# Weaving two self attentions with dense products in a written TensorE order

## The chip, the cores and the metric

The kernel runs on one core of a Trainium2 chip. The metric is the time of one execution on the device in microseconds (us). PE is TensorE (matrix products and transposes), DVE is VectorE, ACT is ScalarE, POOL is GpSimd, SP is the engine whose queue issues most of the DMAs. PSUM is the memory into which PE writes; it has eight banks of 128 x 512 float32 elements.

## The reference

Two transformer layers run one after the other on 512 tokens of width 1024. The first has a feed-forward part, a mixer with three branches, and another feed-forward part; the second layer (a recurrent mixer and a feed-forward part) is not touched. The change lies in the first mixer:

```
(fq, fk, fv, ff, dq, dk, dv, iq, ik, iw, mq, g) = split(rmsnorm(h) @ w_in)
# branch 0, "fox": 8 heads of 64, causal, with forget gates
s = fq . fk / 8 + c_query - c_key,  c = cumsum(log_sigmoid(ff + b_forget))
o_a = softmax(causal(s)) @ fv                    # fq, fk are normalized by head
# branch 1, "dsa": 8 heads of 64, one key and value for all heads
score = sum over 8 heads of iw * relu(iq . ik)   # the indexer
o_b = softmax(dq . dk / 8 over the 128 best keys of each query) @ dv
# branch 2, memory: 4 heads of 128 over 256 memory rows
o_c = softmax(mq . km / sqrt(128)) @ vm
gates = sigmoid(g)                               # 3 x 1024
h = h + (sum over n of gates[n] * (o[n] @ w_branch[n])) @ w_out
```

All inputs and outputs are float32.

## The kernel before, in words

Activations lie feature-major: a tile is 128 features by 512 tokens, and the model's 1024 features are eight such tiles. Every dense product is made of three PE products, because float32 is split into a high and a low part that PE takes in its rounded form fp32r: high x high, high x low, low x high (`mm3`, L163, L168, L169). Weights come by DMA as a `raw` block of 512 KB; ACT rounds it to `whi` (L157), DVE subtracts to get `wlo` (L158), and PE uses such a block in 24 products of 128 x 512. `gemm_fm` runs such products over blocks of 256 output features; its results go into two PSUM banks in turn (tag `g`).

The mixer (`Mix1.run`) goes through these stages: a small product for keys and scalars; the indexer's queries `iq`; the indexer (`pix` products, whose sums DVE gathers); the memory attention; the products for `fv`, `fq`, `fk`; the fox attention; the search for the 128 best keys (`selected`, 48 pairs of MAX8 and MATCH_REPLACE8 on DVE); the memory branch (gates, then the projection, `branch(2)`); the product for `dq` with its norm and rotation (`rope`); the dsa attention; the other two branches; the output product.

An attention is cut into 16 units: four chunks of two heads, times four blocks of 128 queries (`qb`). A unit with `w` = 128 (qb + 1) keys does, for each of its two heads: scores (L584 and L585); a DVE instruction that adds the mask and takes the row maximum (L986 or L1008); the exponential with its row sum on ACT (L689); a reciprocal on DVE (L690); the multiplication by it on POOL (L691); one to four transposes on PE (L679) into the PSUM tile `pt`; a copy on ACT (L681). Then PE multiplies by the values (L697), one product of 64 output rows for each head and block, into the PSUM tile `po`.

A score is two products. The query tile `st` holds a head's high part in the head's own 64 partitions and its low part in the other 64 (`stacked`). The key tile `kh` holds the high part twice. So the first product uses all 128 rows of PE's array. The second multiplies the high part of the query by the low part of the key `kl` and uses 64 rows:

```python
own, w = slice(p * 64, p * 64 + 64), max(w, 256)
self.nc.tensor.matmul(ps[:, :w], q, keys[0][:, :w], start=True, stop=False)
self.nc.tensor.matmul(ps[:, :w], q[own], keys[1][own, :w], start=False, stop=True)
```

The order of the instructions on every engine is made by a list scheduler from the order of the program's text, priorities, its own estimates of durations and the free buffers: it may put PE products of a later stage between those of an attention. Each engine then runs its list in order and waits on semaphores. PSUM banks of the mixer: two for dense products (`g`), one general (`a`), three for scores (`s`), one for `pt` (`p`), one for `po` (`o`).

Of the kernel before, what the change touches and what calls it, by code (L numbers as in the profile page):

```python
# [19 lines left out]
D = 1024  # L20
# [7 lines left out]
class K:  # L28
# [142 lines left out]
    def gemm_fm(self, w, c0, ncols, x, evac, kmax=4, after=None, then=iter(())):  # L171

        nk = len(x)
        for g in range(0, ncols, 256):
# [3 lines left out]
            for k0 in range(0, nk, kmax):  # L180
                kk = min(kmax, nk - k0)
                hi, lo = self.wload([(w[k0 * 128:(k0 + kk) * 128, c0 + g:c0 + g + gc], gc)], kk, gc)
                for (m, mc), ps in zip(ms, pss):
                    for k in range(kk):
                        xh, xl = x[k0 + k]
                        self.mm3(ps[:mc], hi[:, k, m:m + mc], lo[:, k, m:m + mc], xh, xl,
                                 k0 + k == 0, k0 + k == nk - 1, after if k0 + k == 0 else None)
                    if k0 + kk == nk:
                        evac((g + m) // 128, ps[:mc])
                next(then, None)  # L190
# [320 lines left out]
class Mix1:  # L511
# [54 lines left out]
    def doubled(self, x, new, lo):  # L566
# [3 lines left out]
        his = []  # L570
# [9 lines left out]
    def score(self, ps, q, p, keys, w):  # L580
# [25 lines left out]
    def head_stats_turned(self, chunks, heads, width, s):  # L606


        nc, k = self.nc, self.k
        per = 128 // width  # L610
# [3 lines left out]
        for i, c in enumerate(chunks):  # L614
            ps, sq = k.ps("tq", "s"), k.tmp("hq")
            for b in range(NB):
# [3 lines left out]
                                    mybir.AxisListType.X, ALU.add)  # L620
        yv, rt = y.rearrange("p (b h) -> p b h", b=NB), self.rt.unsqueeze(2).to_broadcast([128, NB, heads])
# [5 lines left out]
        return yv  # L627
# [22 lines left out]
    def head_norm_rows(self, chunks, y, gcol):  # L650

# [13 lines left out]
        nc.vector.tensor_sub(z[32:32 + n], ps[:n], z[:n].bitcast(F32))  # L665
        for i, x in enumerate(chunks):
# [4 lines left out]
            else:  # L671
                nc.vector.scalar_tensor_tensor(x, x, gcol, pb, op0=ALU.mult, op1=ALU.mult)

    def transposed(self, p, nb, s):

        nc, k = self.nc, self.k
        pt = k.ps("pt", "p")
# [29 lines left out]
    def run(self):  # L707
# [67 lines left out]
        scores, mq = [], []  # L775
        steps = self.indexer(iq, ik, scores, 4)
        k.gemm_fm(win, 2768, 512, y, raw_evac(mq), then=steps)
        for _ in steps:
            pass
        om = self.mem_attention(mq, self.head_stats_turned(mq, 4, 128, "hm"))  # L780

        fvt = k.sp.tile([128, NB, 512], F32, name="fv")
        k.gemm_fm(win, 1024, 512, y, self.turned_evac(fvt, R))
        fv = [fvt[:, b] for b in range(NB)]
        fq, fk = [], []
        k.gemm_fm(win, 0, 512, y, raw_evac(fq))
        st = self.head_stats_turned(fq, 8, 64, "hs")

        def norm():
            for _ in range(3):  # L790
                yield
            self.head_norm_rows(fq, st, k.c("fqg"))
            yield

        k.gemm_fm(win, 512, 512, y, raw_evac(fk), then=norm())
        self.head_norm_rows(fk, self.head_stats_turned(fk, 8, 64, "hs"), None)
        self.forget()
        of = self.fox(fq, fk, fv)
        bias = self.selected(scores)

        merged = [None] * DC
        self.branch(2, om, merged)

        dq = []
        k.gemm_fm(win, 1544, 512, y, raw_evac(dq, k.tmp))

        rq = self.head_stats_turned(dq, 8, 64, "hm")
        nc.vector.tensor_scalar(k.c("rot"), k.c("rot"), k.c("dqg"), None, op0=ALU.mult)
        nc.vector.tensor_scalar(self.cos, self.cos, k.c("dqg"), None, op0=ALU.mult)
        dq = [self.stacked(t, lambda s: k.slot(s, F32R)) for t in map(self.rope, dq)]  # L810
        od = self.dsa(dq, dk, bias, rq)

        self.branch(0, of, merged)
        self.branch(1, od, merged)
# [83 lines left out]
    def indexer(self, iq, ik, scores, n):  # L898
# [10 lines left out]
        for qb in range(1, NB):  # L909
            w = (qb + 1) * 128  # L910
            acc = k.slot("ix")[:, :w]
            for hh in range(8):
                c, p = hh // 2, hh % 2
                ps = k.ps("pix", "s")[:, :w]
                self.score(ps, iq[c][p][:, qb * 128:(qb + 1) * 128], p, ik, w)
# [11 lines left out]
    def selected(self, scores):  # L927

        k, nc = self.k, self.nc
        bias = [k.c("cmask")]  # L930
        for acc in scores:
            for _ in range(TOPK // 8):
                m8 = k.small("m8", [128, 8], bufs=6)
                nc.vector.max(m8, acc)
                nc.vector.match_replace(acc, m8, acc, TAKEN)
            nc.vector.tensor_scalar(acc, acc, 0.5 * TAKEN, MASK, op0=ALU.is_gt, op1=ALU.mult)
            bias.append(acc)
        return bias
# [18 lines left out]
    def fox(self, fq, fk, fv):  # L957
        k, nc = self.k, self.nc
        out = []

        def made(c):
            return (self.stacked(fq[c], lambda s: k.tmp(s, F32R)),
                    self.doubled(fk[c], lambda s: k.slot(s, F32R), k.tmp("kl", F32R)))

        ahead = made(0)
        for c in range(4):
            po = k.ps("po", "o")
            (q2, (k2, kl)), ahead = ahead, made(c + 1) if c < 3 else None
            nc2 = []
            for p in range(2):  # L970
                nct = k.tmp("nct", tag="nct")
                nc.sync.dma_start(nct, self.nc_rows[2 * c + p:2 * c + p + 1, :].to_broadcast([128, T]))
                nc2.append(nct)

            for qb in reversed(range(NB)):
                w = (qb + 1) * 128
                d = slice(w - 128, w)
                pts = []
                for p in range(2):
                    nct = nc2[p]  # L980
# [828 lines left out]
```

## Time and profile before

| | |
|---|---|
| median of 3 runs | 2288.93 us (2285.36 to 2290.96) |
| the profiled execution | 2286.21 us, its span 2284.5 us |
| busy share of the span | PE 97%, DVE 57%, ACT 38%, POOL 15% |
| mean granted PE clock | 0.990 of full speed |
| chain of work that ended last | PE 87%, DVE 5%, POOL 4% |
| DMA | 202.39 MB, mean 89 GB/s |

The span is from the first to the last instruction; the execution's own time is 1.7 us more. A matrix product's row in the trace lasts longer than the distance to the next product's start, since products are pipelined, so PE shows as busy while products follow each other at any distance below their length. What a product costs is read from start to start. In the stretch from 449.7 us (the first rotation of the mixer) to 939.5 us (where the output product begins) lie all the stages named above from the indexer on.

### The profile page before, as it was taken

Reading aid. Unit: us, or ns where it says so; the run is one execution under the profiler, and the core shown is the slowest. Engines: PE = TensorE matmul, PEld = TensorE weight load, DVE = VectorE, ACT = ScalarE, POOL = GpSimd, SP = SyncE. Lnnn points to the kernel's source line nnn. Section 1 sums busy time; section 2 is a strip of 40 time slices with the busy share of each in tenths; the row PEclk is TensorE's granted clock in tenths of the full one; section 3 lists DMA queues with packets and bytes.
Section 4 is the critical chain, followed back from the end, with each engine's and each line's share of the span. In section 5 each row is a group of like instructions: output and inputs, shape, how many; then the busy total and the mean of one; then the engine's idle time right before and its main releaser. Section 6 shows DMA issues by size and latency. Waiting matters only on the chain.

```text
span 2284.5 us, 27935 instructions
## 1 busy us (share of the span) xinstructions
PE 2224.8 (97%) x10700; PEld 1772.9 (78%) x10700; DVE 1305.4 (57%) x2210; ACT 877.1 (38%) x1485; POOL 346.6 (15%) x349
## 2 busy tenths in 40 slices
PE   8999999999999999999999998999999998999998
PEld 7788888768767578888888877778777787888887
DVE  4544433589763644544443348985888725877623
ACT  4432222345373542332322235543433534444321
POOL 0110100111040421101111012370222200000000
PEclk9999999999999999999999999999999999999999
DMA  4333333312312113333332332331121223333232
GB/s 150 93 111 102 98 100 117 105 44 58 93 56 74 37 47 111 114 90 96 100 94 95 116 108 66 93 109 30 56 73 48 74 93 120 93 95 99 94 99 94
DMA packets 198509, 202.39 MB, mean 89 GB/s; under 512 B 19556, under 2 KB 184063, under 8 KB 198375
## 3 DMA queue, kind: packets, MB, share of 16 engines
q1 hardware_dynamic: 197607, 198.12, 28.9%
q0 software_dynamic: 768, 2.49, 0.4%
q8 instruction: 84, 1.38, 0.3%
q14 instruction: 50, 0.41, 0.1%
HBM read 192.70 MB, written 7.88 MB: 88 GB/s over the span
## 4 chain that ended last, share of the span: by engine, by line
PE 87%; DVE 5%; POOL 4%; issue 1%; ACT 1%; DMA 1%; SPq 0%; POOLq 0%; DVEq 0%; ACTq 0%
PE pg L169 23%; PE pg L163 23%; PE pg L168 23%; PE pd L1739 2%; PE pd L1738 2%; PE pd L1737 2%; PE po L697 1%; POOL blocks L1349 1%; PE pt L679 1%; POOL xt L1348 1%; PE pss L585 1%; DVE wlo L158 1%; PE pyd L1536 1%; PE pss L584 1%; PE tr L1126 1%
## 5 line engine op out<-in xcount | busy, mean ns | idle before, releaser
L163 PE MATMUL pg<-yh,whi 128*128 128x512 f32 x1856 | 737.1, 398 | 4.0 <-ACT yh L219 2.3
L169 PE MATMUL pg<-yh,wlo 128*128 128x512 f32 x1856 | 736.2, 397 | 1.3 <-DVE wlo L158 1.1
L168 PE MATMUL pg<-yl,whi 128*128 128x512 f32 x1856 | 734.8, 396 | 0.0
L158 DVE TENSOR_TENSOR wlo<-raw,whi 128x1024 fp32r<-128x1024 f32 x341 | 422.7, 1240 | 529.2 <-ACT whi L157 518.6
L157 ACT CAST whi<-raw 128x1024 fp32r<-128x1024 f32 x349 | 362.0, 1038 | 701.4 <-PE pg L168 511.6
L169 PEld LDWEIGHTS pg<-yh,wlo 128*128 128x128 f32 x1856 | 351.2, 189 | 78.7 <-issue 5.0
L163 PEld LDWEIGHTS pg<-yh,whi 128*128 128x128 f32 x1856 | 351.4, 189 | 78.0 <-issue 6.0
L168 PEld LDWEIGHTS pg<-yl,whi 128*128 128x128 f32 x1856 | 351.2, 189 | 72.6 <-issue 3.1
L163 PE MATMUL pg<-hidh,whi 128*128 128x512 f32 x352 | 138.9, 394 | 0.0
L169 PE MATMUL pg<-hidh,wlo 128*128 128x512 f32 x352 | 138.1, 392 | 0.0
L355 POOL TENSOR_TENSOR hp<-ut,sg 128x512 f32<-128x512 f32 x44 | 73.3, 1666 | 422.7 <-DVE ut L353 398.0
L168 PE MATMUL pg<-hidl,whi 128*128 128x512 f32 x352 | 136.8, 389 | 0.0
L211 ACT CAST hidh<-hp 128x512 fp32r<-128x512 f32 x44 | 27.3, 620 | 142.4 <-POOL hp L355 142.3
L169 PEld LDWEIGHTS pg<-hidh,wlo 128*128 128x128 f32 x352 | 66.1, 188 | 15.4
L1696 DVE SCALAR_TENSOR_TENSOR fo<-ft,fcw,fo 128x511 f32<-128x511 f32 x88 | 65.8, 749 | 21.2 <-ACT fo L1693 20.0
L168 PEld LDWEIGHTS pg<-hidl,whi 128*128 128x128 f32 x352 | 66.1, 188 | 14.6
L163 PEld LDWEIGHTS pg<-hidh,whi 128*128 128x128 f32 x352 | 66.3, 188 | 13.1
L212 DVE TENSOR_TENSOR hidl<-hp,hidh 128x512 fp32r<-128x512 f32 x44 | 30.4, 691 | 79.5 <-ACT hidh L211 79.5
L1737 PE MATMUL pd<-whi,hidh 128*128 128x512 f32 x176 | 69.5, 395 | 0.0
L1738 PE MATMUL pd<-whi,hidl 128*128 128x512 f32 x176 | 69.5, 395 | 0.0
L1739 PE MATMUL pd<-wlo,hidh 128*128 128x512 f32 x176 | 69.3, 397 | 0.0
L346 DVE TENSOR_TENSOR gt<-pg,R 128x512 f32<-128x512 f32 x44 | 30.3, 692 | 55.2 <-PE pg L169 55.2
(501 smaller groups left out, 3067.7 us busy)
## 6 DMA issues: line engine op xcount, KB each, us to landing
raw<-in_w_in SPq DMA_DIRECT2D x100, 512.0 KB
raw<-in_ffn_w_gate SPq DMA_DIRECT2D x40, 512.0 KB
raw<-in_ffn_w_up SPq DMA_DIRECT2D x40, 512.0 KB
raw<-in_ffn_w_down SPq DMA_DIRECT2D x40, 512.0 KB
raw<-in_w_up SPq DMA_DIRECT2D x40, 512.0 KB
raw<-in_w_out SPq DMA_DIRECT2D x24, 512.0 KB
raw<-in_w_down SPq DMA_DIRECT2D x22, 512.0 KB
raw<-in_w_branch SPq DMA_DIRECT2D x12, 512.0 KB
```

The costliest lines, as they stand in the source:

```text
L157: nc.scalar.copy(hi, raw)
L158: (self.lo or nc.vector).tensor_sub(lo, raw, hi.bitcast(F32))
L163: first = mm(out, whi, xhi, start=start, stop=False)
L168: mm(out, whi, xlo, start=False, stop=False)
L169: mm(out, wlo, xhi, start=False, stop=stop)
L212: nc.vector.tensor_sub(lo, x, hi.bitcast(F32))
L346: nc.vector.tensor_mul(gt, ps, R)
L355: nc.gpsimd.tensor_mul(p, ut, sg[m])
L1696: nc.vector.scalar_tensor_tensor(o[:, s:], t[:, :T - s], k.fcw[:, j:j + 1], o[:, s:], op0=ALU.mult, op1=ALU.add)
L1737: nc.tensor.matmul(pss[b], xh[:, s], hi[:, i], start=st, stop=False)
L1738: nc.tensor.matmul(pss[b], xl[:, s], hi[:, i], start=False, stop=False)
L1739: nc.tensor.matmul(pss[b], xh[:, s], lo[:, i], start=False, stop=sp)
```

## The change

- `score` uses all 128 rows in its second product too. For this `doubled` makes two tiles `kl` for a chunk of keys, one for each head, and copies the low part into the other 64 partitions (on ACT). The indexer's and dsa's keys had both halves filled already.
- `gemm_steps` yields after every three products (one `mm3`), so that dense products can be handed out in small steps.
- The stages before the fox attention come in another order: `mq`, then `fk`, `fq`, `fv`, with the memory attention handed out in steps among them; `forget` moves ahead of `fk`.
- The units of fox and dsa form one list of 32. Inside a block marked `manual_schedule` the PE keeps the order of the text: for each unit the first head's transposes, one step (three products), the second head's transposes, the scores of the next unit, two steps, the unit's values, three steps, and two (fox) or three (dsa) steps more. The other engines are still ordered by the list scheduler. The steps are taken from the memory branch, `dq`, branch 0 and the gates of branch 1.
- The norm, rotation and splitting of `dq` are handed out between units 12 and 16. The two heads' `pt` tiles go to the banks `p` and `a`. Score tiles `s` get four buffers in place of three.

```diff
+    def gemm_steps(self, w, c0, ncols, x, evac, kmax=4, after=None):
...
+                        if k0 + kk == nk and k == kk - 1:
+                            evac((g + m) // 128, ps[:mc])
+                        yield m == ms[-1][0] and k == kk - 1
...
+    def doubled(self, x, new, newlo):
...
         for p in range(2):
-            t = new("kh")
+            t, lo = new("kh"), newlo("kl")
             own, other = (slice(o, o + 64) for o in (p * 64, 64 - p * 64))
             nc.scalar.copy(t[own], x[own])
+            nc.vector.tensor_sub(lo[own], x[own], t[own].bitcast(F32))
             nc.scalar.copy(t[other], t[own].bitcast(F32))
-            nc.vector.tensor_sub(lo[own], x[own], t[own].bitcast(F32))
-            his.append(t)
-        return his, lo
+            nc.scalar.copy(lo[other], lo[own].bitcast(F32))
+            out.append((t, lo))
+        return out
...
-        own, w = slice(p * 64, p * 64 + 64), max(w, 256)
...
+    def score(self, ps, q, keys, w):
...
+        w = max(w, 256)
         self.nc.tensor.matmul(ps[:, :w], q, keys[0][:, :w], start=True, stop=False)
-        self.nc.tensor.matmul(ps[:, :w], q[own], keys[1][own, :w], start=False, stop=True)
+        self.nc.tensor.matmul(ps[:, :w], q, keys[1][:, :w], start=False, stop=True)
...
+        def products():
+            yield from self.branch(2, om, merged)
+            yield from k.gemm_steps(win, 1544, 512, y, raw_evac(dq, k.tmp))
+            yield from self.branch(0, of, merged)
+            for g in range(0, D, 256):
+                yield from self.gates(1, g, "c", gates)
...
+            def between(i):
+                if i == 12:
...
+                    for _ in range(2):
+                        next(stats)
+                if i == 14:
+                    next(stats)
+                    rq.append(next(stats))
+                for c in {14: (0,), 15: (1,), 16: (2, 3)}.get(i, ()):
+                    dq2.append(self.stacked(dq[c], lambda s: k.slot(s, F32R)))
+                for c in {13: (0,), 14: (1,), 15: (2, 3)}.get(i, ()):
+                    self.rope(dq[c])
+            fill(4)
+            units[0].scores()
+            fill(6)
+            for i, u in enumerate(units):
+                u.turn(0)
+                fill(1)
+                u.turn(1)
+                if i + 1 < len(units):
+                    units[i + 1].scores()
+                for _ in range(4):
+                    next(top, None)
+                fill(2)
+                u.values()
+                fill(3)
+                between(i)
+                fill(2 if i < 16 else 3)
+            fill(1000)
+        for g in range(0, D, 256):
+            for _ in self.project(1, g, gates[g // 128:g // 128 + 2], od, merged):
+                pass
```

PE, inside the fox attention, before. `pss` are scores, `pt` transposes, `po` values, `pg` dense products (here of the memory branch):

```order
2659 L697 MATMUL po_4672<-pt_4730,fv 64x128
2660 L679 MATMUL pt_4753<-ct_base,s_4744 128x128 x3
2661 L584 MATMUL pss_4842<-kh_4668,st_4660 128x256
2662 L585 MATMUL pss_4842<-kl_4663,st_4660 128x256
2663 L168 MATMUL pg_5749<-oml_3830,whi_5752 128x512
2664 L169 MATMUL pg_5749<-omh_3829,wlo_5753 128x512
2665 L584 MATMUL pss_4885<-kh_4680,st_4673 128x512
2666 L679 MATMUL pt_4772<-ct_base,s_4763 128x128 x3
2667 L697 MATMUL po_4672<-pt_4757,fv 64x128
2668 L585 MATMUL pss_4885<-kl_4679,st_4673 128x512
2669 L163 MATMUL pg_5749<-omh_3902,whi_5752 128x512
2670 L584 MATMUL pss_4905<-kh_4684,st_4676 128x512
```

The same place in the changed kernel, from the second head's transposes of one unit to the first values:

```order
2685 L703 MATMUL pt_5168<-ct_base,s_5094 128x128 x4
2686 L591 MATMUL pss_5176<-kh_4703,st_4697 128x384
2687 L592 MATMUL pss_5176<-kl_4704,st_4697 128x384
2688 L591 MATMUL pss_5189<-kh_4709,st_4700 128x384
2689 L592 MATMUL pss_5189<-kl_4710,st_4700 128x384
2690 L163 MATMUL pg_5144<-omh_4653,whi_5148 128x512
2691 L168 MATMUL pg_5144<-oml_4654,whi_5148 128x512
2692 L169 MATMUL pg_5144<-omh_4653,wlo_5149 128x512
2693 L163 MATMUL pg_5145<-omh_4000,whi_5148 128x512
2694 L168 MATMUL pg_5145<-oml_4001,whi_5148 128x512
2695 L169 MATMUL pg_5145<-omh_4000,wlo_5149 128x512
2696 L721 MATMUL po_5222<-pt_5163,fv 64x128
```

Scores, transposes and values came singly, with one to four dense products between them, and a unit's values mostly in two parts (one product, then the rest); now both heads' scores stand together, six dense products follow, and a unit's values stand in one group.

ACT where the fox attention starts, before. `st` are split queries, `kh` keys, `s` exponentials, `pt` copies of transposes:

```order
325 L574 CAST kh_4668<-qk_4441 64x512
326 L575 CAST kh_4668<-kh_4668 64x512
327 L1051 ACTIVATE gate_5730<-gt_5728 128x512
328 L574 CAST kh_4680<-qk_4455 64x512
329 L689 ACTIVATE s_4696,den_4701<-s_4696,ng_4698 128x512
330 L157 CAST whi_5788<-raw_5786 128x1024
```

The same place in the changed kernel; `pt_4632` and `pt_4649` belong to the last unit of the memory attention, and `kl` to the first fox unit:

```order
317 L705 COPY pt_4632<-pt_4629 128x256
318 L582 CAST kh_4685<-kh_4685 64x512
319 L580 CAST kh_4691<-qk_3774 64x512
320 L705 COPY pt_4649<-pt_4646 128x256
321 L583 CAST kl_4686<-kl_4686 64x512
322 L582 CAST kh_4691<-kh_4691 64x512
323 L727 CAST omh_4653<-po_4483 128x512
324 L583 CAST kl_4692<-kl_4692 64x512
325 L580 CAST kh_4703<-qk_3788 64x512
```

The copies for the first fox scores stand behind the copies of the memory attention's last unit, and the first exponential (`s_4723`) stands another seven instructions further down, at number 332.

POOL where dsa starts, before. `qk` is a chunk of `dq` in its rotation, `s` the multiplication by the reciprocal:

```order
134 L550 TENSOR_TENSOR qk_6112<-qk_6112,ry_6206 128x512
135 L549 TENSOR_TENSOR qk_6126<-qk_6126,cos_3028 128x512
136 L550 TENSOR_TENSOR qk_6126<-qk_6126,ry_6218 128x512
137 L691 TENSOR_SCALAR s_6232<-s_6232,den_6237 128x128
138 L691 TENSOR_SCALAR s_6248<-s_6248,den_6253 128x128
```

And in the changed kernel, where `s_6226` and `s_6238` are the two heads of dsa's first unit:

```order
133 L715 TENSOR_SCALAR s_6226<-s_6226,den_6231 128x128
134 L555 TENSOR_TENSOR qk_6135<-qk_6135,cos_3028 128x512
135 L556 TENSOR_TENSOR qk_6135<-qk_6135,ry_6276 128x512
136 L555 TENSOR_TENSOR qk_6153<-qk_6153,cos_3028 128x512
137 L715 TENSOR_SCALAR s_6238<-s_6238,den_6243 128x128
138 L556 TENSOR_TENSOR qk_6153<-qk_6153,ry_6282 128x512
```

The last two rotations now stand between the two heads of dsa's first unit.

## Rows read from the trace of the kernel before

**Rows 1.** The page: busy us (share) x instructions; chain that ended last by engine.
```profile
PE 2224.8 (97%) x10700; PEld 1772.9 (78%) x10700; DVE 1305.4 (57%) x2210; ACT 877.1 (38%) x1485; POOL 346.6 (15%) x349
...
PE 87%; DVE 5%; POOL 4%; issue 1%; ACT 1%; DMA 1%; SPq 0%; POOLq 0%; DVEq 0%; ACTq 0%
```

**Rows 2.** Busy time by stage: from:to, length, engines' busy us, granted clock, DMA.
```profile
472.70:583.00 110.30, 110.13 (x521) 83.71 (x520) 102.97 (x279) 54.52 (x110) 10.23 (x19) 1.00 0.20 58
...
741.70:762.20 20.50, 16.95 (x58) 10.41 (x56) 17.90 (x35) 8.20 (x13) 8.62 (x7) 0.83 0.09 27
```

**Rows 3.** PE in order of time, indexer: start us, length us, instruction.
```profile
497.61 0.40 PE L584 MATMUL pix<-kh,st 128*128 128x512 f32 x1
497.94 0.49 PE L585 MATMUL pix<-kl,st 64*128 64x512 f32 x1
498.36 0.50 PE L168 MATMUL pg<-yl,whi 128*128 128x512 f32 x1
498.70 0.40 PE L169 MATMUL pg<-yh,wlo 128*128 128x512 f32 x1
498.93 0.40 PE L584 MATMUL pix<-kh,st 128*128 128x512 f32 x1
```

**Rows 4.** Groups of 64-row score products from 449 to 940 us.
```profile
L585 PE MATMUL pss<-kl,st 64*128 64x256 f32 (+2 forms) x64 | 27.2, 431 | 0.0
...
L585 PE MATMUL pix<-kl,st 64*128 64x256 f32 (+2 forms) x24 | 10.7, 445 | 0.0
```

**Rows 5.** PE in order of time, dense products 256 wide; and all LDWEIGHTS of L163.
```profile
111.12 0.28 PE L163 MATMUL pg<-my,whi 128*128 128x256 f32 x1
111.24 0.28 PE L168 MATMUL pg<-my,whi 128*128 128x256 f32 x1
...
L163 PEld LDWEIGHTS pg<-yh,whi 128*128 128x128 f32 x1856 | 351.4, 189 | 78.0 <-issue 6.0
```

**Rows 6.** PE in order of time, values of dsa (two records each).
```profile
779.88 0.43 PE L697 MATMUL po<-pt,tm 128*64 128x128 f32 x2
780.24 0.50 PE L169 MATMUL pg<-ofh,wlo 128*128 128x512 f32 x1
780.58 0.39 PE L163 MATMUL pg<-ofh,whi 128*128 128x512 f32 x1
...
785.49 1.09 PE L697 MATMUL po<-pt,tm 128*64 128x128 f32 x14
```

**Rows 7.** Waits of PE from 449 to 940 us: total, times, longest.
```profile
PE pss L584 <- DVE st L562: 1.8, 1, 1.8
PE rot L546 <- DVE ry L548: 1.7, 1, 1.7
...
PE pt L679 <- POOL s L691: 0.5, 1, 0.5
```

**Rows 8.** DVE and PE in order of time, first head of fox.
```profile
627.66 0.68 DVE L986 CUSTOM_DVE_ANT_0 s<-pss,nct 128x512 f32<-128x512 f32 x1
...
632.67 0.60 PE L679 MATMUL pt<-ct_base,s 128*128 128x128 f32 x4
```

**Rows 9.** Groups by shape from 449 to 940 us: busy us, mean ns, idle before.
```profile
L157 ACT CAST whi<-raw 128x1024 fp32r<-128x1024 f32 x57 | 59.8, 1050 | 120.0 <-PE pg L168 112.0 <-issue 8.0
...
L690 DVE RECIPROCAL den<-den 128x1 f32<-128x1 f32 x80 | 12.7, 159 | 12.2 <-ACT s L689 11.5
L550 POOL TENSOR_TENSOR qk<-qk,ry 128x512 f32<-128x512 f32 x8 | 12.6, 1579 | 12.3 <-DVE ry L548 3.4 <-DVE hst L230 3.4 <-DVE ng L1010 2.1
...
L691 POOL TENSOR_SCALAR s<-s,den 128x512 f32<-128x512 f32 x16 | 11.1, 692 | 13.1 <-DVE den L690 4.4 <-DVE ng L1010 3.0 <-DVE ng L987 1.5
...
L549 POOL TENSOR_TENSOR qk<-qk,cos 128x512 f32<-128x512 f32 x8 | 10.7, 1335 | 49.7 <-ACT hq L618 45.1 <-ACT st L561 2.9 <-PE rot L546 1.6
...
L689 ACT ACTIVATE s<-s,ng 128x512 f32<-128x512 f32 x8 | 5.8, 723 | 1.9 <-DVE ng L987 1.1 <-DVE den L690 0.8
...
L575 ACT CAST kh<-kh 64x512 fp32r<-64x512 f32 x8 | 4.9, 617 | 0.2
```

**Rows 10.** PE's granted clock in one stretch: length, PE busy, clock.
```profile
755.30:762.10 6.80, 6.80 (x14) 0.50 0.00 0
```

More of the change, by code (lines that the diff above doesn't have):

```diff
@@ L171, in gemm_fm @@
     def gemm_fm(self, w, c0, ncols, x, evac, kmax=4, after=None, then=iter(())):
+        for end in self.gemm_steps(w, c0, ncols, x, evac, kmax, after):
+            if end:
+                next(then, None)
+    def gemm_steps(self, w, c0, ncols, x, evac, kmax=4, after=None):
         nk = len(x)
@@ L613, in head_stats_turned @@
         xv = x.rearrange("p (b h) -> p b h", b=NB)
-        for i, c in enumerate(chunks):
+        for i in range(n_chunks):
+            c = chunks[i]
             ps, sq = k.ps("tq", "s"), k.tmp("hq")
@@ L774, in run, with first @@
             iq[i] = self.stacked(self.rope(iq[i]), new)
-        scores, mq = [], []
-        steps = self.indexer(iq, ik, scores, 4)
-        k.gemm_fm(win, 2768, 512, y, raw_evac(mq), then=steps)
+        scores, mq, om, fq, fk = [], [], [], [], []
+        fvt = k.sp.tile([128, NB, 512], F32, name="fv")
+        fv = [fvt[:, b] for b in range(NB)]
+        def first():
+            yield from self.indexer(iq, ik, scores, 4)
+            yield from self.mem_attention(mq, self.head_stats_turned(mq, 4, 128, "hm"), om)
@@ new lines, in after @@
+        def after(n, stats, chunks, gcol):
+            for _ in range(n):
+                next(steps, None)
+                yield
+            self.head_norm_rows(chunks, stats, gcol)
+            yield
+            while True:
+                next(steps, None)
+                yield
+        steps = first()
+        k.gemm_fm(win, 2768, 512, y, raw_evac(mq, lambda s: k.slot(s, tag="o")), then=steps)
+        self.forget()
+        k.gemm_fm(win, 512, 512, y, raw_evac(fk), then=steps)
+        st = self.head_stats_turned(fk, 8, 64, "hs")
@@ L778, in run @@
+        k.gemm_fm(win, 0, 512, y, raw_evac(fq), then=after(2, st, fk, None))
+        st = self.head_stats_turned(fq, 8, 64, "hs")
+        k.gemm_fm(win, 1024, 512, y, self.turned_evac(fvt, R), then=after(2, st, fq, k.c("fqg")))
         for _ in steps:
             pass
[L780 to L799, printed above, removed]
@@ L814, in run, with fill @@
-        self.branch(1, od, merged)
+        of, od, dq, gates, merged = [], [], [], [], [None] * DC
+        def products():
[4 more added lines that the diff above has]
+                yield from self.gates(1, g, "c", gates)
+        work = products()
+        def fill(n):
+            for _ in range(n):
+                next(work, None)
@@ new lines, in run @@
+        bias = [k.c("cmask")]
+        top = self.selected(scores, bias)
+        with self.tc.manual_schedule(engines={mybir.EngineType.PE}):
+            units = self.fox(fq, fk, fv, of)
+            dq2, rq = [], []
+            units += self.dsa(dq2, dk, bias, rq, od)
+            stats = self.stats_steps(dq, 8, 64, "hm", 4)
+            def between(i):
+                if i == 12:
+                    nc.vector.tensor_scalar(k.c("rot"), k.c("rot"), k.c("dqg"), None, op0=ALU.mult)
+                    nc.vector.tensor_scalar(self.cos, self.cos, k.c("dqg"), None, op0=ALU.mult)
+                    for _ in range(2):
[24 more added lines that the diff above has]
+            fill(1000)
@@ L955, in forget, with fox, at @@
         nc.sync.dma_start(self.nc_rows, c[:8])
-    def fox(self, fq, fk, fv):
+    def fox(self, fq, fk, fv, out):
         k, nc = self.k, self.nc
-        out = []
+        class Chunk:
+            pass
         def made(c):
[L962 to L969, printed above, removed]
+            x = Chunk()
+            x.q = self.stacked(fq[c], lambda s: k.tmp(s, F32R))
+            x.k = self.doubled(fk[c], lambda s: k.slot(s, F32R),
+                               (lambda s: k.hslot(s, F32R)) if c < 2 else (lambda s: k.slot(s, F32R)))
+            return x
+        ahead = {}
+        def at(c):
+            for i in (c, c + 1):
+                if i < 4 and i not in ahead:
+                    ahead[i] = made(i)
+            x = ahead[c]
+            x.nct, x.po = [], None
             for p in range(2):
@@ L972, in fox, with unit, scores @@
                 nc.sync.dma_start(nct, self.nc_rows[2 * c + p:2 * c + p + 1, :].to_broadcast([128, T]))
[L973 to L978, printed above, removed]
+                x.nct.append(nct)
+            return x
+        def unit(c, qb):
+            w = (qb + 1) * 128
+            d = slice(w - 128, w)
+            u = Chunk()
+            def scores():
+                x = u.x = at(c) if qb == NB - 1 else ahead[c]
+                u.s, u.pt = [], []
                 for p in range(2):
-                    nct = nc2[p]
+                    nct = x.nct[p]
                     nc.gpsimd.tensor_add(nct[:, d], nct[:, d], k.c("cmask"))
                     ps = k.ps("pss", "s")
-                    self.score(ps, q2[p][:, d], p, (k2[p], kl), w)
+                    self.score(ps, x.q[p][:, d], x.k[p], w)
                     s = k.tmp("s", tag="s")
```

152 lines of the change are left out of this document (88 added, 64 removed).

## The prediction, as it was made

> **What bounds the kernel now.** I read the page first. PE is busy in 2224.8 of 2284.5 us [rows 1], and the chain of work that ended last lies on it for 87% [rows 1]. So a gain has to come out of PE's own time, or out of the few places where PE waits. The next view is busy time by stage over the part that the change touches, 449.7 to 939.5 us. From 472.7 to 583.0 PE is busy for 110.13 of 110.30 us, and DVE for 102.97, because the search for the best keys runs there beside the indexer and the memory attention [rows 2]. The list of waits shows that PE hardly waits in this part: the longest waits from the fox attention on are 1.8 and 1.7 us, both just ahead of dsa [rows 7]. After them the granted clock is 0.50 for 6.8 us [rows 10], the lower level of 1.2 GHz.
>
> If PE neither waits nor is short of work, the question is what its busy time is made of. That takes the timeline, from start to start. Dense products of 512 columns follow each other at 0.23 us (the last two starts of [rows 3]). A score pair in the same stretch goes: 64-row product 0.33 us after the 128-row one, next product 0.42 us later, the one after it another 0.34 us later [rows 3]. Where 0.68 us would do for three products, these take 1.09. Each passage between products on 128 and on 64 rows thus costs about 0.2 us, half before and half behind it, and a pair in dense work has two. The trace counts the pair as busy all the while, so the page's 97% hides it.
>
> **The change part by part.**
>
> *Second score product on all rows.* Two passages a pair, 1.09 - 0.68 = 0.41 us; I take 0.39, a little under. There are 64 pairs in the two attentions and 24 in the indexer [rows 4]: 88 x 0.39 = 34 us. Some pairs share a passage with a neighbour that also changes the array's shape, so this is near the upper end; the lower is 25 us. That a full 128-row product of 256 columns can follow another with different weights at 0.12 us is shown by the memory product, although its weight load lasts 189 ns [rows 5]: loads are hidden.
>
> *Values in one group.* A lone value product (two records) holds PE for 0.36 us, and the second dense product behind it comes after 0.34 in place of 0.23 [rows 6]; seven last 1.09 against 0.43 for one, so a product itself is worth 0.11. The fixed part of a group is thus 0.36 - 0.11 + 0.11 = 0.36 us, and some 0.1 ahead of it. In the written orders values form 61 groups before and 32 after. 29 x 0.46 = 13 us is the upper end; about half of the old groups touch transposes or 64-row products, with which they share the passage, so I take 8, and 5 as the lower end.
>
> *Transposes.* Their number stays; more of the groups now stand between dense products. +1.5 us, from 0 to 3.
>
> *The passage to dsa.* Before, the chain norm, rotation, splitting of `dq` ran just ahead of the first dsa scores. It cost the waits of 1.8 and 1.7 us, one of 0.5 for POOL [rows 7], and the slow stretch: 6.8 us at half clock [rows 10] do the work of 3.4. The change spreads that chain over units 12 to 16. Removed: 1.8 + 1.7 + 0.5 + 3.4 = 7.4 us.
>
> Removed in all: 34 + 8 - 1.5 + 7.4 = 48 us. Now what is added.
>
> *DVE ahead of fox.* The search for keys still stands ahead of the first fox scores in DVE's list; handing it out four pairs a unit did not move it. In 472.7 to 583.0 PE's work shrinks by some 20 pairs x 0.39 = 8 us, to 102 us, while DVE keeps its 103 [rows 2]. DVE then has no slack and what is late is the norm of `fq`, so I add 3 us (0 to 8).
>
> *The start of fox.* PE's order is fixed there: last transposes and values of the memory attention, then four scores, 18 dense products, the first transposes. ACT's list has, ahead of the second head's last key half, some ten instructions of about 0.6 us (617 ns for a key half [rows 9]) which themselves wait for PE's two memory transposes. From the end of the last product of that norm (`hb`) I count along the lists: DVE's norm, a split weight and two maxima 3.5 us, exponential and reciprocal with three query splits between them 2.4, POOL and the transposes 1, then seven ACT copies 4.4: 11.5 us, against 5.5 us of PE work in the same rows. So 6 us of waiting. The first exponential stands behind six more key copies and a weight cast of 1050 ns [rows 9], 4.8 us, then 0.72 exponential, 0.16 reciprocal, 0.69 POOL [rows 9]: 6.3 us against 18 x 0.23 = 4.1 of dense products, 2 us more. The norm of `fq` ahead of it waits likewise about 2. Sum 10 us (4 to 14). Waits of that size were followed by a slow stretch before [rows 7, 10], so I add one more, 3.4 us (0 to 7).
>
> *The passage to dsa, new.* On POOL the last rotations (1335 and 1579 ns each [rows 9]) stand between the two heads of dsa's first unit, and DVE's and ACT's splits of those chunks wait for them ahead of the next unit's maxima and copies. 1.2 us at the second head's transposes, 1.5 at the values, 1 in the unit before: 4 us (1 to 7).
>
> *The other units.* From a unit's scores to its first transposes PE has 21 or 24 dense products (4.8 or 5.5 us) and the values (0.4 to 1.2). The chain they must cover is maximum 0.68, exponential 0.72, reciprocal 0.16, multiplication 0.69 [rows 8, 9]: 2.3 us if nothing stands in the way, and 5.0 us as the first fox head really took it, from 627.66 to 632.67 with other work in the queues [rows 8]. Both ends lie at or under the cover; I add 2 us for all 30 (0 to 20). The eight extra key copies on ACT (617 ns) hide under its 38% load, save at the start of fox, where they are counted.
>
> Added: 3 + 10 + 3.4 + 4 + 2 = 22, and net 48 - 22 = 26 us. Against the profiled execution's 2286.2 us this gives 2260 us. The median of the runs shown is 2288.9, by 2.7 more; runs lie 5.6 apart. I say 2260.
>
> **The rivals.**
>
> *A, most of the new waits are hidden.* If the start of fox costs 4 us without a slow stretch and the rest the low ends, 48 - 5 = 43: 2243 us. For it speaks that the lists were made by a scheduler that saw these dependencies; against it that its durations are estimates.
>
> *B, the units wait.* Each engine runs its list in order, so a weight cast or an evacuation ahead of a link holds the whole chain. If the chain takes 6 us as a rule, each of 30 units waits about 0.6: 18 us more, 2278 us. For it speak the 5.0 us of [rows 8]; against it that there the order held heads back that PE did not yet need.
>
> *C, the other side: PE's clock falls again and again.* Place: the transposes of a unit that come 2 us late. Price: the wait and 3.4 us for the slow stretch, 5.4 together. The gain of 26 us is gone at five such units of 32; with eight it is 2286 - 26 + 43 = 2303 us. Against it: waits under 1 us were not followed by a slow stretch in this part, and B's waits are below that.
>
> *D, the second product's price stays.* If the 0.39 us came from the two tiles or the changing weights and not from the 64 rows, 34 us fall out of the sum: 2294 us. Against it: products of 128 rows in rows 5 have none of it.
>
> *E, full-row weight loads aren't hidden.* If each second product waits 0.19 us for its load, 88 x 0.19 = 17 us come back: 2277 us. The row of 0.12 us start to start speaks against it. The Trainium skill, "TensorE: Matmul & The Clock Gate", Part 3, The mechanism, says that a weight load overlaps products in flight only when its row group differs, which 64 and 128 rows do not offer here; by that rule this rival would hold. The trace of before disagrees for equal rows: loads of 189 ns stand in products 0.12 us apart.
>
> **How the numbers follow.** Forecast (2251 to 2269) 0.48; A 0.19; B 0.14; C 0.08; D 0.07; E 0.04. The likeliest gives 2260. The range is to leave out 2 in 10: C and D lie above, and some of A's lower and B's upper ends, so 2240 to 2281. The measurement tells changes over 0.3% from none, which is 6.9 us (2282.1 to 2295.8). The forecast, A, B and E are faster: 0.85. D is the same: 0.07, and C is slower: 0.08.
>
> **What would show it.** Right: 128 rows in all score products, next to each other at 0.12 to 0.23 us; the output product begins 25 us earlier; PE waits at the start of fox by 6 to 12 us in total, for ACT copies (`kl`, `kh`) and POOL (`s`); DVE near 100% in the 50 us before fox. Wrong: starts 0.3 us apart between full-row score products (D or E); waits for POOL `s` in most units (B), or a granted clock of 0.50 in more than three stretches there (C). What would make the number most wrong is the start of fox, where 10 + 3.4 us are counted along lists and not read from rows.

## The result and the profile after

The changed kernel takes 2261.5 us (median of 4 runs, 2258.0 to 2263.9) against 2288.9 for the kernel before: a ratio of 0.988, 95% interval 0.986 to 0.990, so 27 us less. The prediction was 2260. The profiled execution's span is 2258.9 us, 25.6 less than before's.

The page of the changed kernel, as in [rows 1]:

```profile
PE 2186.8 (97%) x10700; PEld 1764.9 (78%) x10700; DVE 1296.9 (57%) x2210; ACT 881.6 (39%) x1493; POOL 347.2 (15%) x349
...
PE 84%; DVE 9%; POOL 2%; ACT 2%; issue 2%; DMA 0%; SPq 0%; POOLq 0%; DVEq 0%; ACTq 0%
```

PE's share is still 97%, with 38 us less of busy time in 25.6 us less of span. On the chain that ended last, PE's share has fallen from 87 to 84% and DVE's has risen from 5 to 9%: the kernel now waits for other engines a little more.

PE in order of time in a fox unit of the changed kernel (columns as in [rows 3]):

```profile
694.10 0.36 PE L591 MATMUL pss<-kh,st 128*128 128x256 f32 x1
694.30 0.28 PE L592 MATMUL pss<-kl,st 128*128 128x256 f32 x1
694.41 0.28 PE L591 MATMUL pss<-kh,st 128*128 128x256 f32 x1
694.53 0.28 PE L592 MATMUL pss<-kl,st 128*128 128x256 f32 x1
694.65 0.39 PE L163 MATMUL pg<-omh,whi 128*128 128x512 f32 x1
694.88 0.40 PE L168 MATMUL pg<-oml,whi 128*128 128x512 f32 x1
```

The second head's two products and the dense product behind them follow at 0.12 us. The output product (`mgh`) begins at 912.94 us, 25.7 earlier than before, where it began at 938.62 (the 939.5 given for it above is 0.9 too late). So the gain lies in the stages that the prediction named. Before, then after:

```profile
938.62 0.40 PE L163 MATMUL pg<-mgh,whi 128*128 128x512 f32 x1
912.94 0.39 PE L163 MATMUL pg<-mgh,whi 128*128 128x512 f32 x1
```

All waits of PE from 449 to 940 us in the changed kernel (total, times, longest), to set beside [rows 7]:

```profile
PE pt L703 <- POOL s L715: 6.2, 4, 2.1
PE pix L591 <- DVE st L568: 3.3, 2, 2.8
PE pss L1146 <- ACT s L713: 2.4, 1, 2.4
PE tq L633 <- ACT qk L744: 1.9, 2, 1.0
PE pg L163 <- DVE pj L1186: 1.5, 2, 1.3
PE rot L552 <- DVE ry L554: 1.3, 1, 1.3
PE po L1155 <- ACT pt L705: 1.0, 2, 0.5
PE pix L591 <- ACT ixt L990: 0.4, 1, 0.4
PE pss L592 <- ACT kl L583: 0.3, 1, 0.3
```

That is 18 us in all, where before had 7. Of those 7, 2.8 lie ahead of the indexer's first product and are not in [rows 7]:

```profile
PE pix L584 <- DVE st L562: 2.8, 1, 2.8
```

The changed kernel has the same wait: the 2.8 in its second row. Of its 6.2 us for POOL's `s`, 3.7 lie at the start of fox, 2.1 at the passage to dsa. And these are busy times by stage and around the places at half clock (columns as in [rows 2]; the third number from the end is the granted clock):

```profile
472.70:560.00 87.30, 84.00 (x399) 66.19 (x397) 83.39 (x227) 41.55 (x79) 7.54 (x14) 0.98 0.25 70
560.00:604.00 44.00, 41.32 (x206) 30.91 (x206) 40.48 (x98) 22.55 (x47) 6.20 (x10) 1.00 0.21 61
605.10:611.90 6.80, 6.37 (x16) 4.85 (x17) 4.01 (x10) 6.08 (x11) 1.29 (x2) 0.50 0.00 0
751.90:755.30 3.40, 3.38 (x10) 1.81 (x9) 2.42 (x9) 2.48 (x7) 0.24 (x1) 0.50 0.00 0
530.00:533.40 3.40, 3.40 (x16) 2.89 (x15) 2.96 (x10) 1.90 (x7) 1.40 (x3) 0.50 0.25 56
```

DVE is busy for 95% of the first stage and for 92% of the second, and PE now stands still in the first for 3.3 us. Three stretches at 0.50 (1.2 GHz) follow waits of 2.0 to 2.4 us: 3.4 us are lost in the one at the start of fox (605.10) and 1.7 in each of the others (half their length). Before had one of 6.8 us here [rows 10]. The product at 462 us, the indexer's first, is followed by one of 6.8 us in both kernels.

### The profile page after: what moved, and what is told of

It reads as the page before. It is cut to its first block, busy times and chain, and to the rows that moved or that the text cites. A ratio compares the mean times of both kernels' runs of the same rounds, so it can differ in the third digit from the quotient of the medians.

```text
span 2258.9 us, 27897 instructions
## 1 busy us (share of the span) xinstructions
PE 2186.8 (97%) x10700; PEld 1764.9 (78%) x10700; DVE 1296.9 (57%) x2210; ACT 881.6 (39%) x1493; POOL 347.2 (15%) x349
## 4 chain that ended last, share of the span: by engine, by line
PE 84%; DVE 9%; POOL 2%; ACT 2%; issue 2%; DMA 0%; SPq 0%; POOLq 0%; DVEq 0%; ACTq 0%
PE pg L163 23%; PE pg L169 23%; PE pg L168 23%; PE pd L1871 2%; PE pd L1869 2%; PE pd L1870 2%; DVE wlo L158 1%; PE po L721 1%; PE pt L703 1%; ACT whi L157 1%; PE pyd L1668 1%; PE tr L1258 1%; POOL hp L361 1%; DVE ix L994 1%; DVE ix L1007 1%
## 5 line engine op out<-in xcount | busy, mean ns | idle before, releaser
L163 PE MATMUL pg<-yh,whi 128*128 128x512 f32 x1856 | 740.9, 400 | 4.0 <-ACT yh L225 2.3
L163 PEld LDWEIGHTS pg<-yh,whi 128*128 128x128 f32 x1856 | 351.1, 189 | 79.6 <-issue 8.1
L163 PE MATMUL pg<-hidh,whi 128*128 128x512 f32 x352 | 138.7, 394 | 0.0
L169 PEld LDWEIGHTS pg<-hidh,wlo 128*128 128x128 f32 x352 | 66.1, 188 | 15.5
L163 PEld LDWEIGHTS pg<-hidh,whi 128*128 128x128 f32 x352 | 66.2, 188 | 13.1
L715 POOL TENSOR_SCALAR s<-s,den 128x256 f32<-128x256 f32 (+3 forms) x80 | 43.2, 542 | 207.9 <-DVE den L714 159.1
```

Of the source, the lines that this page charges most:

```text
L163: first = mm(out, whi, xhi, start=start, stop=False)
L169: mm(out, wlo, xhi, start=False, stop=stop)
L715: nc.gpsimd.tensor_scalar(p[:, :w], p[:, :w], den, 1.0, op0=ALU.mult, op1=ALU.mult)
```

## The experiments

The theory going in: the gain is the passages between 128 and 64 rows, and the values' groups; what it is reduced by are the waits at the start of fox, at the passage to dsa and where DVE is full. The rivals: the second product's price lies elsewhere, or the written order itself makes the gain. The kernel before was run beside each of these kernels; its medians there lie between 2288.4 and 2290.4 us.

**1. The 64 rows put back into the changed kernel.**

```diff
+        own = slice(p * 64, p * 64 + 64)
-        self.nc.tensor.matmul(ps[:, :w], q, keys[1][:, :w], start=False, stop=True)
+        self.nc.tensor.matmul(ps[:, :w], q[own], keys[1][own, :w], start=False, stop=True)
```

> The changed kernel, but the second score product again takes only the head's own 64 rows of query and low key part; both key tiles are still made, nothing else differs. Theory (each passage between products on 128 and on 64 rows costs TensorE about 0.2 us, two a pair, 88 pairs): 25 to 34 us come back, 2286 to 2295 us, about as slow as the kernel before, and a pair's second product is followed 0.4 us later again. Rival (the price lay in the two tiles or the changing weights, and the new order of the stages carries the gain): within 5 us of 2261.

Measured: 2288.2 us, 1.0002 of before (0.9991 to 1.0013). The whole gain of 27 us is gone, as the theory had it. The same unit, PE in order of time:

```profile
708.26 0.36 PE L591 MATMUL pss<-kh,st 128*128 128x256 f32 x1
708.55 0.38 PE L593 MATMUL pss<-kl,st 64*128 64x256 f32 x1
708.87 0.38 PE L591 MATMUL pss<-kh,st 128*128 128x256 f32 x1
709.18 0.38 PE L593 MATMUL pss<-kl,st 64*128 64x256 f32 x1
709.49 0.50 PE L163 MATMUL pg<-omh,whi 128*128 128x512 f32 x1
709.82 0.39 PE L168 MATMUL pg<-oml,whi 128*128 128x512 f32 x1
```

From the first `kh` to the second dense product it takes 1.56 us, against 0.78 (694.10 to 694.88) above: 0.39 a pair, as the prediction had it.

**2. Rows alone, in the old order.**

```diff
-        own, w = slice(p * 64, p * 64 + 64), max(w, 256)
+        w = max(w, 256)
-        self.nc.tensor.matmul(ps[:, :w], q[own], keys[1][own, :w], start=False, stop=True)
+        self.nc.tensor.matmul(ps[:, :w], q, keys[1][:, :w], start=False, stop=True)
```

> The kernel before with one part of the change alone: the second score product on all 128 rows, with the two low key tiles and their copies that it needs; the order of the text, the four stages and the three score buffers stay as before. Theory (the rows carry the gain, the order costs about what it brings): 24 to 34 us faster than before, 2255 to 2265 us, so beside the changed kernel. Rival (the weave of units and dense products carries the gain): at most 10 us faster than before, above 2278 us.

Measured: 2281.3 us, 0.997 (0.996 to 0.998). Only 7 us: the theory is refuted, and the number is the rival's. The rival's reason isn't shown by it, since in experiment 1 the weave without the rows brings nothing. The waits of PE from 610 to 640 us, and two stretches of its windows:

```profile
PE pss L585 <- ACT kh L576: 6.5, 1, 6.5
PE pss L585 <- DVE mx L988: 2.1, 2, 1.1
PE pss L586 <- ACT kl L577: 0.5, 1, 0.5
```

```profile
619.00:625.80 6.80, 4.15 (x8) 2.23 (x8) 6.16 (x11) 6.48 (x12) 1.09 (x2) 0.51 0.60 190
629.20:632.60 3.40, 3.40 (x11) 2.07 (x10) 1.24 (x6) 2.31 (x6) 1.71 (x3) 0.52 0.00 0
```

PE saves its time and reaches the first fox scores before ACT has copied the keys (ACT is busy for 6.48 of 6.80 us there). It waits 9 us, where the kernel before waits 0.5, and up to 5 us go to the lower clock (half of 6.8 and of 3.4; the first of these stretches begins while PE still waits). So in the old order the rows' gain turns into waits.

**3. The same with the new order of the stages ahead of fox.**

```diff
-        k.gemm_fm(win, 1024, 512, y, self.turned_evac(fvt, R))
-        k.gemm_fm(win, 0, 512, y, raw_evac(fq))
-        k.gemm_fm(win, 512, 512, y, raw_evac(fk), then=norm())
+        self.forget()
+        k.gemm_fm(win, 512, 512, y, raw_evac(fk), then=steps)
+        k.gemm_fm(win, 0, 512, y, raw_evac(fq), then=after(2, st, fk, None))
+        k.gemm_fm(win, 1024, 512, y, self.turned_evac(fvt, R), then=after(2, st, fq, k.c("fqg")))
```

> The kernel before with the second score product on all rows (2281.3 us when measured alone) and with one more part of the change: the stages ahead of fox in the new order (mq, fk, fq, fv, the memory attention handed out among them, forget ahead of fk). The units of fox and dsa and the products behind them keep the old text; values still form 61 groups. Theory (of the gain that rows alone missed, the larger part was lost where fox starts, where 11 us of waits for the keys' copies and queries and 5 us by the slow clock had come up): 8 to 14 us faster than 2281, 2267 to 2273 us. Rival (that gain is in the weave of the units and in their 32 groups of values; the start of fox only moves its wait): within 4 us of 2281, 2277 to 2285 us.

Measured: 2272.5 us, 0.993 (0.991 to 0.994), 9 us less than rows alone, which is in the theory's range. PE's waits from 600 to 640 us no longer name the keys:

```profile
PE pt L680 <- POOL s L692: 1.7, 3, 0.9
PE pt L680 <- ACT pt L682: 0.6, 1, 0.6
PE po L698 <- ACT pt L682: 0.5, 2, 0.2
```

The remaining 11 us down to 2261.5 come with the weave of the units.

**4. The values in two groups.**

```diff
                 fill(2)
-                u.values()
-                fill(3)
+                u.values(0)
+                fill(1)
+                u.values(1)
+                fill(2)
```

> The changed kernel with each unit's values in two groups: the first product, one step of three dense products, then the rest; 64 groups in place of 32, and the steps of a unit otherwise as many as before. Theory (a group has a fixed cost of 0.25 to 0.46 us): 8 to 15 us slower, 2269 to 2276 us. Rival (a group costs nothing beside its products): within 3 us of 2261, and then the 8 us that the prediction put on the groups were elsewhere.

Measured: 2275.9 us, 0.994 (0.992 to 0.996), 14.4 more than the changed kernel, or 0.45 us for each of the 32 groups added; the theory's range reached from 0.25 to 0.46. PE in a unit of one block, whose two products now stand apart:

```profile
709.21 0.39 PE L169 MATMUL pg<-yh,wlo 128*128 128x512 f32 x1
709.53 0.43 PE L723 MATMUL po<-pt,fv 128*64 128x128 f32 x2
709.89 0.50 PE L163 MATMUL pg<-yh,whi 128*128 128x512 f32 x1
710.23 0.39 PE L168 MATMUL pg<-yl,whi 128*128 128x512 f32 x1
```

From the dense product ahead to the second one behind it: 1.02 us for a group of one product, where two dense distances are 0.46. A product is worth 0.11, so the group's own price is 0.45, against the 0.46 read from [rows 6].

**5. No written order.** TensorE's order is left to the list scheduler; the text stays.

```diff
-        with self.tc.manual_schedule(engines={mybir.EngineType.PE}):
+        with ExitStack():
```

> The changed kernel without the block that makes TensorE keep the order of the text: its order too comes from the list scheduler, which stays close to the text (33 groups of values in place of 32, transposes of some units one by one between dense products). Theory (what decides is how products follow each other, which hardly differs): within 4 us of 2261. Rival (the written order itself carries the gain): over 10 us slower, above 2271 us.

Measured: 2251.3 us, 0.983 (0.982 to 0.985), 10 us less than the changed kernel. Neither theory nor rival: the written order costs 10 us. The start of fox shows it, in order of time on PE: first without the written order, then in the changed kernel:

```profile
601.61 0.44 PE L703 MATMUL pt<-ct_base,s 128*128 128x128 f32 x2 [0.88 <-POOL s L715]
601.80 0.48 PE L169 MATMUL pg<-yh,wlo 128*128 128x512 f32 x1
...
602.81 0.61 PE L1155 MATMUL po<-pt,vm 128*128 128x128 f32 x4
```

```profile
602.61 0.44 PE L703 MATMUL pt<-ct_base,s 128*128 128x128 f32 x2 [2.03 <-POOL s L715]
603.51 0.71 PE L1155 MATMUL po<-pt,vm 128*128 128x128 f32 x4 [0.46 <-ACT pt L705]
...
605.20 1.22 PE L1155 MATMUL po<-pt,vm 128*128 128x128 f32 x4 [0.53 <-ACT pt L705]
```

The scheduler puts dense products between the late links, which the written order keeps for behind the scores. It waits less (1.5 us from 601 to 617, where the changed kernel waits 5.0), and its clock stays at full speed there:

```profile
604.00:608.00 4.00, 4.00 (x19) 2.83 (x18) 2.96 (x6) 3.90 (x7) 1.37 (x1) 1.00 0.00 0
```

**6. A longer lead at the start of fox, with the written order.**

```diff
-            fill(4)
+            fill(12)
             units[0].scores()
-            fill(6)
+            fill(8)
...
-                fill(2 if i < 16 else 3)
+                fill(1 if i < 10 else 2 if i < 16 else 3)
```

> The changed kernel with a longer lead where fox starts: 12 steps of dense products ahead of the first scores in place of 4, and 8 behind them in place of 6; the units 0 to 9 give back one step each, and from unit 10 on all stands as before. Theory (the start of fox costs 5 us of waits at the changed kernel's profile, and 3.4 us by the slow clock that followed them): 5 to 9 us faster than the changed kernel's 2261, 2252 to 2257 us, and no granted clock of 0.5 between 604 and 615 us. Rival (the steps given back make the units wait in their turn, or the keys' copies are late whatever stands ahead): within 3 us of 2261.

Measured: 2256.4 us, 0.986 (0.984 to 0.988), 5 us less by the medians, the theory's lower end (the two kernels' intervals overlap a little). PE waits 2.4 us there in place of 5.0, at full clock:

```profile
612.00:616.00 4.00, 2.45 (x12) 1.69 (x12) 2.06 (x5) 3.98 (x9) 1.11 (x2) 1.00 0.04 11
```

**7. The search for the best keys beside the fox units.**

```diff
-                nc.vector.max(m8, acc)
+                first = nc.vector.max(m8, acc)
+                k.tc.add_manual_dep(first.ins, self.last.ins.name, ...)
```

`last` is the newest score product; the dependency only orders the scheduler's list and adds no wait.

> The changed kernel with the search for the best keys held back in DVE's list: each of its 48 pairs comes behind the score products of the unit in which the text hands it out, so that it runs beside the fox units and no longer beside the memory attention. Theory (DVE without slack ahead of fox costs a wait of 2.4 us, the slow stretch of 1.7 us behind it, and part of the late start of fox): 3 to 6 us faster than 2261, 2255 to 2258 us. Rival (the pairs, now between the maxima of the fox units, hold up 48 times what those units wait for): 2 to 10 us slower, 2263 to 2271 us.

Measured: 2257.6 us, 0.987 (0.985 to 0.988), 4 us less by the medians, as much as the theory had; here too the intervals overlap. The wait of 2.4 us in the memory attention is gone, and DVE has air in that stage (busy 53.35 us in place of 83.39):

```profile
472.70:560.00 87.30, 85.71 (x411) 67.30 (x411) 53.35 (x117) 43.31 (x83) 9.72 (x15) 1.00 0.23 70
```

The waits as a whole do not fall, though: taken as in the table further down they are 15.3 us (15.5 in the changed kernel), since those for POOL's `s` rise from 6.2 to 8.1, and the start of fox waits 5.3 in place of 5.0. What falls is the loss by the lower clock, from 9.9 to 5.1.

**8. Later rotations of `dq`.**

```diff
-                for c in {14: (0,), 15: (1,), 16: (2, 3)}.get(i, ()):
+                for c in {14: (0,), 15: (1,), 19: (2,), 20: (3,)}.get(i, ()):
...
-                for c in {13: (0,), 14: (1,), 15: (2, 3)}.get(i, ()):
+                for c in {13: (0,), 14: (1,), 18: (2,), 19: (3,)}.get(i, ()):
```

> The changed kernel with the rotations of the chunks 2 and 3 of dq handed out in units 18 and 19, their splits in 19 and 20, in place of 15 and 16, so that they no longer stand in POOL's list between the two heads of dsa's first unit. Theory (at the passage to dsa, 745 to 755 us, 3.4 us of waits and 1.7 us by the slow clock come from those rotations): 2 to 5 us faster than 2261, 2256 to 2259 us. Rival (the first two chunks' rotations alone already make PE wait there): within 2 us of 2261.

Measured: 2260.9 us, 0.988 (0.987 to 0.990), no change in the time, as the rival had it. Yet the trace shows what the theory said at its place. Of the 3.4 us of waits between 735 and 760 us, 1.7 stay, and the stretch at half clock behind them is gone:

```profile
PE pt L703 <- POOL s L715: 1.7, 2, 1.0
```

```profile
748.00:752.00 4.00, 3.86 (x21) 2.96 (x22) 1.95 (x9) 2.07 (x6) 1.05 (x3) 1.00 0.44 131
```

The wait for the rotation (`ry`) is gone, and that for POOL's `s` gets shorter. A wait of 0.9 for `tq` that falls into these 25 us here is in the changed kernel too, at 734 us. From the indexer's first product to the output product this execution takes 447.5 us, 3.0 less than the changed kernel's; outside of that stretch it takes 3.9 more, where the lower clock alone costs 5.0 more. So the rival's reason, waits that stay, is not what the trace shows, and a gain of 2 or 3 us is neither shown by the medians nor excluded.

**9. Together.** The free order with the late search, then also with the late rotations or with the longer lead.

> The changed kernel with both: TensorE's order left to the list scheduler (2251.3 us when measured alone), and the search held back behind the score products of the fox units. Theory (what remained of waits ahead of fox, 2.4 us, goes too): 2 to 5 us faster than 2251, 2246 to 2249 us. Rival (the scheduler had already hidden what DVE's load costs, or the fox units now wait for DVE): 2250 to 2258 us.

> The changed kernel with TensorE's order left to the scheduler, the search held back beside the fox units (these two: 2246.2 us), and the late rotations of two chunks of dq. Theory (the passage to dsa still has 1.9 us of waits there, which the late rotations took to 0 to 1 us with the written order): 1 to 3 us faster than 2246, 2243 to 2245 us. Rival (as with the written order, what is won at the passage is given back behind it): within 1.5 us of 2246.

> The changed kernel with TensorE's order left to the scheduler, the search held back (2246.2 us for these two), and the longer lead where fox starts (12 and 8 steps). Theory (the scheduler already draws dense products ahead of the late transposes, so a longer lead finds under 1 us of waits to remove): within 2.5 us of 2246. Rival (the start of fox still costs time that no wait shows): 3 to 6 us faster, 2240 to 2243 us.

Measured: 2246.2 (0.982, 0.980 to 0.984), 2244.5 (0.981, 0.979 to 0.982) and 2250.6 us (0.983, 0.981 to 0.985). The search gives 5 us more than the free order alone by the medians, as expected. The rotations' 1.7 is within the scatter and can't be told from nothing. The lead brings nothing on top: the rival is out, and the median lies 4.4 us above 2246.2, outside the theory's 2.5 too. The runs behind it lie 10 us apart, so that it costs time is not shown. The fastest beats both kernels, by 44 us and 17.

## Why the prediction was right

The terms are of two kinds: what PE's own products take, and what PE loses by waiting and by the lower clock. They can be told apart. Take the length from the indexer's first product to the first output product. Subtract the waits that the list of waits gives in it (without the 2.8 us ahead of that first product, which all have), and the loss by the clock (the length of a stretch times one minus its granted clock). What is left is PE's own time. All kernels have the same dense products in this length. Gaps under 0.15 us are not in the list and stay in PE's own time; they come to 0.3 to 0.5 us in these kernels.

| kernel (us, profiled execution) | length | waits | clock | PE's own |
|---|---|---|---|---|
| before | 477.6 | 4.5 | 6.8 | 466.3 |
| before, rows alone (2) | 469.0 | 20.5 | 6.8 | 441.7 |
| before, rows and stages (3) | 460.6 | 13.4 | 3.4 | 443.8 |
| changed | 450.5 | 15.5 | 9.9 | 425.1 |
| changed, 64 rows (1) | 480.0 | 12.9 | 10.2 | 456.9 |
| changed, values split (4) | 466.0 | 17.6 | 5.1 | 443.3 |
| changed, free order (5) | 437.9 | 10.2 | 1.7 | 426.0 |

A wait that falls into a stretch at half clock is taken off twice. That matters in experiment 2 alone: 1.4 us, which makes its own time 443.1; elsewhere it is at most 0.2.

*PE's own time.* Predicted: 34 for the rows, 8 for the values, 1.5 given back for transposes, -40.5 in all. Shown: -41.2. Rows 128 take off 31.8 in the new order (456.9 to 425.1), 0.36 for each of 88 pairs. The rest is 466.3 - 456.9 = 9.4 against 6.5 predicted for values and transposes; it also holds what the new order does to the pairs' passages. So the size is near, and the reason for the discount from 13 to 8 is not shown. The prediction had about half of the old groups of values touch transposes or 64-row products; in the order of before 54 of 61 do, and 22 of them have no dense product on either side. Split anew in experiment 4, 32 groups cost 18.2 of PE's own time, 0.57 each (waits and clock there are 2.7 lower).

*Waits and clock.* Predicted: -7.4 for the old passage to dsa and +22.4 for the new places, +15. Shown: waits +11.0, clock +3.1, so +14.1. That this sum came out is luck. By places, predicted first: start of fox 13.4, shown 8.4 (waits of 5.0, half of 6.8 at half clock); passage to dsa 4, shown 5.1 (2.1, 1.3 and half of 3.4); DVE full ahead of fox 3, shown 4.1 (2.4 and half of 3.4), though the late link was an exponential of the memory attention and not the norm of `fq`; other units 2, shown 3.4 (the waits of 1.9 for `qk` and 1.5 for `pj`, which the prediction didn't name). One place was too dear and three too cheap. At the start of fox the prediction saw 6 us for the keys' copies on ACT, and PE waited 0.3 for `kl`. Its sign of being right, 6 to 12 us of waits there, was missed with 5.0, and DVE was busy for 92% from 560 to 604 us, not near 100%. The count along ACT's list was too long; what is late there is POOL's `s` (3.7), of the memory attention's last unit and of the first fox unit, and the `pt` copies (1.0).

*The rivals.* A, most waits hidden (2243), did not come about; the free order goes part of the way, to 2251. B is out: from 619 to 745 us PE waits only for `qk`, and for no unit's `s`. C's mechanism, a wait of 2 us with a stretch at half clock behind it, is there, with three stretches at half clock from the memory attention on, not eight. D is refuted by experiment 1. E too: `kl`, `kh`, `kl` and a dense product follow at 0.11 to 0.12 us from 694.30 on, though a weight load lasts 189 ns [rows 5]. The two products of [rows 5] that the prediction read share their weights `whi`; here the second head's `kh` and the dense product bring others. The Trainium skill, "TensorE: Matmul & The Clock Gate", Part 3, The mechanism, says in its list that loads overlap products in flight only where the row group differs, while its opening paragraph also excepts loads into a background weight buffer; the list's rule, taken alone, does not agree with these traces. Its page "TensorEngine Tiling (Array Packing)", Tiling Modes, Key Properties, says that a change of the tiling mode drains TensorE; the 0.39 us a pair agree with that, and no run here shows more of its cause.

*What it didn't see* is that the terms depend on each other. Rows alone bring 7 us, all the rest alone nothing (experiment 1 stands at before's time), both together 27. In the old order full rows take 23.2 us from PE's own time (466.3 to 443.1), 0.26 a pair against 0.36 in the new; and 16 come back as waits, 9 of them at the start of fox. That pairs in the old order share passages with values explains a part at most: 16 of the 88 64-row products stand next to a value product there, which at 0.2 us a passage makes 3 of the 8.6 us. The new stages take 7 of these waits and 3.4 of the clock away (experiment 3). The weave takes 18.7 us off PE's own time, from 443.8 to 425.1, and gives 8.6 back in waits and clock. The written order accounts for those: without it PE's own time is the same within 1 us, and waits and clock are 13.5 lower. Some 12 of these lie behind 602 us, where PE's two orders first differ (16.9 against 5.0); ahead of it PE's order is the same in both.

Open: how the weave's 18.7 us divide between values, transposes and the passages that pairs no longer share, and what the fourth score buffer and the second bank for `pt` add; no run separates them.

## What to carry to other kernels

Read a product's price from start to start: a share of 97% busy hid 27 us of passages between 128 and 64 rows. When a saturated engine is made faster, follow its list to the first place where an input is due; the gain is kept only as far as the engines that feed it are ahead there. Before an order is fixed by hand, run the same text with the scheduler's order: here the stages (9 us) and the weave (11) were worth having, the fixing (10) was not.

## What the hardware did that was not expected

A wait of the same length and place is followed by half clock in one kernel and not in another. The memory attention's scores wait for ACT by 2.37 us in the changed kernel, and the clock is 0.50 from 530.0 to 533.4; without the written order, where PE's list is the same up to this place and beyond, they wait 2.38 us, and it stays at full speed:

```profile
528.99 0.70 PE L1146 MATMUL pss<-km,qk 128*128 128x256 f32 x2 [2.38 <-ACT s L713]
```

```profile
528.00:531.40 3.40, 1.71 (x10) 1.17 (x10) 3.37 (x14) 2.35 (x7) 0.59 (x2) 1.00 0.00 0
531.40:534.80 3.40, 3.38 (x26) 2.89 (x26) 2.99 (x9) 2.46 (x7) 2.03 (x4) 1.00 0.54 154
```

So the loss by the clock, 1.7 to 10 us in the table above, can't be summed from the waits alone. What decides it was not found.
